# A decoder block on one core: the opening unit fed in half tiles, a fourth plain unit, the closing unit in token pieces, norms by a ones product

## The chip, the core and the metric

The kernel runs on one core of a Trainium2 chip. The metric is the device time of one execution in microseconds (us); of each kernel several executions are timed and the median is taken. One further execution is profiled, and its rows are the ones shown below.

## What is computed

One layer of a hybrid decoder block on x (2048 tokens, width 1024, float32), cut to its products and norms:

```python
u = rms_norm(h, norm1_gain)
x_lru, g_lru, q, k, v, g_ret = split(u @ w_in)            # 1024 -> 6 * 512
hl = rg_lru(causal_conv4(x_lru))                          # gates by 64x64 heads, linear scan over tokens
y_lru = rms_norm(hl * gelu(g_lru), lru_norm_gain)
y_ret = head_norm(retention(rotary(q), rotary(k), v)) * silu(g_ret)   # chunks of 128 tokens, 4 heads
h = h + concat(y_lru, y_ret) @ w_out
u = rms_norm(h, norm2_gain)
a, b = split(causal_conv3(u @ ffn_up_w))                  # 1024 -> 2 * 3072
h = h + (gelu(a) * b) @ ffn_down_w
out = rms_norm(h, final_norm_gain)                        # rms_norm: y * rsqrt(mean(y*y) + 1e-6) * gain
```

## The kernel before

Channels lie on the 128 partitions and tokens along the row. The 2048 tokens are two groups g of HT = 1024; a tile ("slot") is 128 x 1024 float32, a product tile in PSUM ("bank") 128 x 512. The work is a list of stages (`order`, line 1427): A and AS (input projection, 12 units per group), B (output projection, 4 units), U (up projection, 24 units), D (down projection, three parts of 4 units per group, the last of them D of g = 1, c = 2). A unit gives two output tiles of 128 channels by 1024 tokens.

Every float32 operand is split into two float32r parts (`split`, line 478: ScalarE casts the high part, VectorE subtracts for the low part), and each block product is three matmuls per 128 channels of contraction (wh·bh, wh·bl, wl·bh). There are two kinds of unit:

- `Unit` (line 551) does a Winograd form of Strassen: 7 products of 12 matmuls 128x512 (84 in all), with sums of weights made on VectorE and sums of data blocks read from DRAM (`Blocks`, line 365: the names 11, T1, T2, 21, T3, T4, 22).
- `PlainUnit` (line 674) does 8 products of 12 matmuls (96 in all), on blocks 11, 12, 21, 22 alone. It needs no sums. The first PLAIN = 3 units of stage A of group 0 and all of stage B are plain.

In the plain units of stage A the raw x is multiplied, with the norm's gain in the split of the block (`RawStage.bring`, line 527); the factor 1/rms of each token (`rb1`) is applied when a bank is emptied (`PlainOut.quadrant`, line 753), so no bank is emptied before `rb1` is there. Five banks (tags x, y, y, e, e) take the quadrants in turn. `norm1` (line 968) makes `rb1` from eight token-major tiles xt of x: Square with a row sum on ScalarE, a power -0.5 on GpSimd, and `spread` (line 906: a diagonal of 8 blocks on VectorE, 8 ones products on TensorE, two copies). `make_x` (line 948) then makes the normalised x and its block sums for the Winograd units.

The other norms (twice over the LRU group, twice over B's output, twice over D's) add up squares in a tile (`SumSq`, line 879) and call `rstd` (line 923): 8 products of a 128-column block with one column of ones, a VectorE step, the power on GpSimd, and `spread` again.

The order of all this is made by a planner (`Flow`, line 173). Every piece of work is a process that yields instructions with a priority, which is a due time in ticks of one product; the planner estimates when an instruction could start and fixes, for each engine, an order by readiness and priority. On the chip each engine keeps that order. SP issues all DMAs, also in that order. Slots (`SLOTS` = 50) and banks are granted by priority too; four more tiles of 128x1040 (tag "w") serve the convolutions' inputs (three or two columns of the tokens before stand ahead of them), residuals, one sum of squares, and the rotary swap. The mask and the retention states of the heads share one slot (`mst`).

At the start (`setup`, line 419) WARM = 10 products of a zero tile run on TensorE. At the end, the last unit is a Winograd unit; its two output tiles are squared, summed, and go through `rstd`, and then `normed` (line 1310) scales eight tiles of 128x1024 and sends each out.

Of the kernel before, what the change touches and what calls it, by code (L numbers as in the profile page):

```python
# [30 lines left out]
P = 128  # L31
# [9 lines left out]
W = 1040  # L41
SLOTS = 50
BANKS = {"x": 1, "y": 2, "e": 2, "sm": 3, "w": 4}
# [5 lines left out]
PLAIN = 3  # L49
SOON = 2  # L50
ISSUE = 0.45
NDUE = 0
LESS = 2
XSTEP = 5
# [3 lines left out]
LAST_PLAIN = False  # L58
WARM = 10
# [12 lines left out]
ANY_TABLE = (AF.Copy, AF.Identity, AF.Square)  # L72

# [16 lines left out]
class Engine:  # L90
# [5 lines left out]
    def __getattr__(self, op):  # L96
        fn = getattr(self.real, op)

        def describe(*args, **kw):
            aps = [x for x in list(args) + list(kw.values()) if isinstance(x, bass.AP)]  # L100
            out = kw.get("out", args[0] if args else None)
            writes = [out.tensor.name]
            if "accum_out" in kw:
                writes.append(kw["accum_out"].tensor.name)
            reads = [x.tensor.name for x in aps if x is not out]
# [67 lines left out]
class Flow:  # L173
# [27 lines left out]
    def free(self, *tiles):  # L201

        for t in tiles:
            name = t.tensor.name
            t1 = max(self.read.get(name, (0,))[0], self.wrote.get(name, (0,))[0])
            self.leaving.append((t1, self.tag.pop(name)))
# [97 lines left out]
def hymba_block_kernel(ctx: ExitStack, tc: tile.TileContext, xh, xn, win, wout, wup, down, gates, vecs,  # L304
# [7 lines left out]
    ev = ctx.enter_context(tc.tile_pool(name="ev", bufs=BANKS["w"]))  # L312
# [7 lines left out]
    def make_bank(tag, name):  # L320
        if tag == "w":
            return ev.tile([P, W], F32, tag="w", name=name)
        return ps.tile([P, Q], F32, tag=tag, name=name, bufs=BANKS[tag])

# [13 lines left out]
    def dma(dst, src):  # L338
        n = 1
        for d in dst.shape:  # L340
            n *= d
        return Op("sp", lambda: nc.sync.dma_start(dst, src), ISSUE, [dst.tensor.name], [src.tensor.name], kb=n / 256)
# [22 lines left out]
    class Blocks:  # L365
# [5 lines left out]
        def __init__(self, name):  # L371
# [35 lines left out]
    big = {}  # L407
# [20 lines left out]
    def constants():  # L428
        yield v.memset(cst, -0.5)
        mst = yield Slot("mst")  # L430
        big["msk"], big["state"] = mst[:, 0:Q], mst[:, Q:HT]
        for t in (ctail, ftail, hlast, mst[:, Q:HT]):
            yield v.memset(t, 0.0)
        for n, t, src in (("idt", idt, ident), ("sml", sml, small),
                          ("msk", mst[:, 0:Q].rearrange("p (a b) -> p a b", b=P), mask)):
            yield dma(t, src)
            have[n].on = True
        yield 0
# [28 lines left out]
    g_d = [[Blocks(f"g{g}_{c}") for c in range(3)] for g in range(NG)]  # L467
# [52 lines left out]
    class RawStage(Stage):  # L520
# [6 lines left out]
        def bring(self, name, i, need, start):  # L527
# [11 lines left out]
            else:  # L539
                hi = yield Slot("bh", F32R)  # L540
                for m in range(2):
                    yield a.activation(hi[:, half(m)], r[:, half(m)], AF.Copy, scale=col(self.gain + 4 * i + 2 * m + k))
                lo = yield Slot("bl", F32R)
                for m in range(2):
# [129 lines left out]
    class PlainUnit:  # L674
# [5 lines left out]
        count = 0  # L680

        def __init__(self, stage, wsrc, out):
            self.stage, self.wsrc, self.out = stage, wsrc, out
            self.w = {}
            self.there = [Event(), Event()]
# [8 lines left out]
        def weights(self, t0):  # L694
            self.t0 = t0

            def one(i, need):
# [6 lines left out]
                self.there[i].on = True  # L704

            fl.spawn(one(0, t0), t0 - 7)
            n1 = t0 + 2 * [m for m, n in self.quads].index(1)
            fl.spawn(one(1, n1), n1 - 7)
# [7 lines left out]
        def part(self, q, m, n, k):  # L716
# [3 lines left out]
            yield self.there[m]  # L720
            bname = f"{k + 1}{n + 1}"
            for j in range(2):
                yield self.stage.event(bname, j)
            wh, wl = self.w[m]
            op = None
            for j in range(4):
                bh, bl = self.stage.blk[bname, j // 2]
                c = half(j % 2)
                ws = slice((4 * k + j) * P, (4 * k + j + 1) * P)
                for i, (x, y) in enumerate(((wh, bh), (wh, bl), (wl, bh))):  # L730
                    mm = pe.matmul(self.ps, x[:, ws], y[:, c], start=k == 0 and j == 0 and i == 0,
                                   stop=k == 1 and j == 3 and i == 2)
                    op = op + mm if op else mm
            yield op
            self.stage.used(bname)
            if k == 1:
                if m not in [x for x, _ in self.quads[q + 1:]]:
                    free(*self.w[m])
                fl.spawn(self.out.quadrant(m, n, self.ps), self.t0 + 2 * q + 4 - SOON)


    class PlainOut:


        off = off2 = 0
        rows = ("slot", "slot")

        def tile(self, i):
            name = f"o{i}"
            t = yield (Bank("w", name) if self.rows[i] == "wide" else Slot(name))  # L750
            return t

        def quadrant(self, m, n, ps):
# [5 lines left out]
            else:  # L759
                q[m] = None  # L760
                q[m] = yield from self.tile(m)
                there.on = True
            off = (self.off, self.off2)[m] + n * Q
            if self.unit.stage.kind == "A":
                yield rb_there[self.g]
                yield v.tensor_tensor(out=q[m][:, off:off + Q], in0=ps, in1=rb1[self.g][:, half(n)], op=ALU.mult)
                rb_used(self.g)
            else:
                yield a.copy(q[m][:, off:off + Q], ps)
# [10 lines left out]
        def u2(self):  # L780
            u = self.unit
            self.t1 = yield from self.tile(0)
            yield a.copy(self.t1[:, self.off + Q:self.off + HT], u.y)
            u.done["u2"].on = True

        def c11(self):
            u = self.unit
            yield u.done["u2"]
            yield a.copy(self.t1[:, self.off:self.off + Q], u.x)
# [3 lines left out]
        def c22(self):  # L793
            u = self.unit
            self.t2 = yield from self.tile(1)
            t = self.t2[:, self.off2 + Q:self.off2 + HT]
# [6 lines left out]
        def c21(self):  # L803
            u = self.unit
            yield a.copy(self.t2[:, self.off2:self.off2 + Q], u.y)
# [4 lines left out]
        def c12(self):  # L810
            u = self.unit
            t = self.t1[:, self.off + Q:self.off + HT]
# [5 lines left out]
    class AddOut:  # L818


        def __init__(self, src, done, wide=True):
            self.src, self.done, self.wide = src, done, wide
# [3 lines left out]
        def load(self, t0):  # L826
            def fn(i):
                yield Until(t0 - 8)
                t = yield (Bank("w", "res") if self.wide else Slot("res"))
                self.t[i] = t[:, 0:HT]  # L830
# [11 lines left out]
        def quadrant(self, m, n, ps):  # L842
# [3 lines left out]
            if (m, 0) in self.quads and (m, 1) in self.quads:  # L846
                yield from self.done(m, self.t[m])

# [30 lines left out]
    class SumSq:  # L879


        def __init__(self, n, wide=False):
            self.acc, self.left, self.wide = None, n, wide

        def add(self, src):
            if self.acc is None:
                acc = yield (Bank("w", "sqacc") if self.wide else Slot("sqacc"))
                self.acc = acc[:, 0:HT]
# [657 lines left out]
```

## Time and profile before

| | us |
|---|---|
| median of 3 executions | 2239.53 (2236.61 to 2242.26) |
| the profiled execution, its time | 2237.51 |
| its span, first to last instruction | 2235.7 |
| TensorE busy in it | 2182.8 |
| VectorE busy | 1780.7 |
| ScalarE busy | 1136.8 |
| mean granted TensorE clock | 0.986 of full |

The span is measured inside the profiled execution; 1.8 us of its time lie outside the span. PE is TensorE's matmuls, PEld its weight loads, DVE VectorE, ACT ScalarE, POOL GpSimd, SPq the DMA-issuing queue of SyncE. Matmul records overlap (a 128x512 record lasts 0.39 us where the next starts 0.23 us later), so rates are read from start to start. A float32 matmul leaves two records.

### The profile page before, as it was taken

The page shows a single profiled execution, that of the slowest core. Times are in us where ns is not written, and L with a number is a line of the kernel's source. Part 1 is how long each engine was busy: PE and PEld are TensorE (multiplying, and loading weights), DVE is VectorE, ACT ScalarE, POOL GpSimd, SP SyncE. Part 2 cuts the span into 40 slices and gives each one's busy share as a digit, 9 for nine tenths or more (in the row PEclk, how much of TensorE's full clock was granted, in tenths as well). Part 3 has the DMA queues.
Part 4 walks back from the last instruction along what each step waited for, and adds up shares of the span by engine and source line. Part 5 has one row for each costly group of instructions (what it writes and reads, how often), then busy time and mean ns, then how long its engine had stood idle before and what let it go on. Part 6 is the DMA issues. An engine that isn't in the chain of part 4 may idle for free.

```text
span 2235.7 us, 26267 instructions
## 1 busy us (share of the span) xinstructions
PE 2182.8 (98%) x9880; PEld 1796.9 (80%) x9880; DVE 1780.7 (80%) x2266; ACT 1136.8 (51%) x1578; POOL 39.7 (2%) x28
## 2 busy tenths in 40 slices
PE   8998999999999999999999999999999999999996
PEld 6877778888788888888888878888888788887884
DVE  7988779777675688899878897878788887788775
ACT  5674666565633155555555755555556444434431
POOL 0000000000000000000000000000000000000000
PEclk9999999999999999999999999999999999999998
DMA  9955263322646872445323532323226677679641
GB/s 356 340 187 196 94 228 135 97 97 94 193 176 238 302 270 95 156 159 179 113 94 137 207 114 99 112 100 102 99 100 224 216 268 285 242 288 370 242 181 75
DMA packets 136063, 405.90 MB, mean 182 GB/s; under 512 B 15232, under 2 KB 16512, under 8 KB 135936
## 3 DMA queue, kind: packets, MB, share of 16 engines
q1 hardware_dynamic: 135936, 404.23, 51.3%
q8 instruction: 77, 1.26, 0.2%
q14 instruction: 50, 0.41, 0.1%
HBM read 272.04 MB, written 123.73 MB: 177 GB/s over the span
## 4 chain that ended last, share of the span: by engine, by line
PE 91%; DVE 4%; DMA 2%; ACT 2%; issue 0%; SPq 0%; POOLq 0%; DVEq 0%; ACTq 0%
PE py L111 33%; PE px L111 22%; PE pe L111 21%; PE pq L111 10%; PE po L111 1%; PE sc L111 1%; DVE res L111 1%; PE pt L111 1%; DVE wl L111 1%; DMA w<-in_dram 1%; PE pk L111 1%; PE pb L111 1%; PE mst L111 0%; PE pa L111 0%; PE pg L111 0%; DVE o L111 0%
## 5 line engine op out<-in xcount | busy, mean ns | idle before, releaser
L111 PE MATMUL py<-bh,wh 128*128 128x512 f32 x744 | 292.8, 394 | 8.4 <-ACT wh L111 6.8
L111 PE MATMUL pe<-bh,wh 128*128 128x512 f32 x744 | 296.6, 399 | 1.0 <-DVE o L111 1.0
L111 PE MATMUL py<-bh,wl 128*128 128x512 f32 x744 | 292.1, 393 | 3.6 <-DVE wl L111 3.6
L111 PE MATMUL px<-bh,wl 128*128 128x512 f32 x744 | 290.6, 391 | 2.3 <-DVE wl L111 2.3
L111 PE MATMUL px<-bh,wh 128*128 128x512 f32 x744 | 291.9, 392 | 0.5 <-DVE res L111 0.5
L111 PE MATMUL pe<-bl,wh 128*128 128x512 f32 x744 | 291.6, 392 | 0.7 <-DVE bl L111 0.7
L111 PE MATMUL pe<-bh,wl 128*128 128x512 f32 x744 | 291.6, 392 | 0.0
L111 PE MATMUL py<-bl,wh 128*128 128x512 f32 x744 | 291.4, 392 | 0.0
L111 PE MATMUL px<-bl,wh 128*128 128x512 f32 x744 | 289.9, 390 | 0.0
L111 ACT CAST wh<-s 128x1024 fp32r<-128x1024 f32 x186 | 195.5, 1051 | 151.2 <-DVE s L111 130.6
L111 DVE SCALAR_TENSOR_TENSOR c<-o,vec,c 128x1024 f32<-128x1024 f32 x192 | 245.9, 1282 | 15.7 <-ACT c L111 12.8
L111 PE MATMUL py<-bh,wv 128*128 128x512 f32 x744 | 248.8, 395 | 3.4 <-ACT bh L111 1.9
L111 DVE TENSOR_TENSOR wl<-s,wh 128x1024 fp32r<-128x1024 f32 x186 | 227.0, 1220 | 29.1 <-ACT wh L111 15.2
L111 ACT COPY o<-py 128x512 f32<-128x512 f32 x207 | 121.5, 587 | 194.2 <-PE py L111 184.9
L111 DVE TENSOR_TENSOR bl<-raw,bh 128x1024 fp32r<-128x1024 f32 x156 | 186.6, 1219 | 2.8 <-ACT bh L111 2.8
L111 ACT ACTIVATE c<-o,vec 128x1024 f32<-128x1024 f32 x96 | 119.7, 1247 | 130.7 <-DVE o L111 130.7
L111 ACT CAST bh<-raw 128x1024 fp32r<-128x1024 f32 x156 | 159.9, 1049 | 40.8 <-DMA raw<-g_T 10.1
L111 PEld LDWEIGHTS py<-bh,wh 128*128 128x128 f32 x744 | 140.7, 189 | 39.5 <-ACT wh L111 8.1
L111 PEld LDWEIGHTS py<-bh,wl 128*128 128x128 f32 x744 | 140.7, 189 | 35.2 <-DVE wl L111 5.8
L111 PEld LDWEIGHTS py<-bh,wv 128*128 128x128 f32 x744 | 140.7, 189 | 34.8 <-ACT bh L111 2.3
L111 PEld LDWEIGHTS pe<-bh,wh 128*128 128x128 f32 x744 | 141.0, 190 | 31.4 <-issue 1.7
L111 PEld LDWEIGHTS pe<-bl,wh 128*128 128x128 f32 x744 | 141.0, 189 | 31.4 <-issue 1.7
(135 smaller groups left out, 3744.2 us busy)
## 6 DMA issues: line engine op xcount, KB each, us to landing
wa<-in_dram SPq DMA_DIRECT2D x93, 512.0 KB, 4.3
wb<-in_dram SPq DMA_DIRECT2D x93, 512.0 KB, 4.3
h<-res SPq DMA_DIRECT2D x56, 512.0 KB, 3.9
g_T<-t SPq DMA_DIRECT2D x96, 256.0 KB, 2.5
raw<-g_T SPq DMA_DIRECT2D x48, 512.0 KB, 6.6
res<-h SPq DMA_DIRECT2D x48, 512.0 KB, 4.6
g<-c SPq DMA_DIRECT2D x72, 256.0 KB, 3.5
raw<-g SPq DMA_DIRECT2D x36, 512.0 KB, 6.8
```

What stands on the lines that cost most here:

```text
L111: return Op(self.name, lambda: fn(*args, **kw), us, writes, reads, func=func)
```

## The change

- Opening: of the first unit, the first weight tile is loaded and split in halves, the wait for blocks stands ahead of each half block, and instructions go out per half block. The second block tile is asked for before the split. The xt loads are due three ticks later (NDUE 0 to 3), constants at tick 3 instead of -5, softplus at 6 instead of 0; warm-up products fall from 10 to 3. The loads of `make_x` no longer wait for `rb1`.
- PLAIN 3 to 4: the fourth unit of stage A of group 0 (its second LRU unit) is plain.
- Closing: the last unit is a `LastUnit`: a plain unit in token ranges 0-512, 512-768, 768-1024. Each range is added, squared, summed, normalised and sent out on its own.
- `rstd`: two float32 products of a 128x128 ones tile with the sum of squares (128x512 each), a ScalarE Sqrt, a VectorE reciprocal.
- All tiles are slots: SLOTS 50 to 54, the four wide tiles go. The convolutions work on 1024 columns and correct the first two or three columns separately (UpOut: three ACT instructions on one column instead of one copy; LruOut: three more small VectorE instructions, one copy less). The mask is one 128x128 tile, the states pass from group 0 to group 1 through DRAM, the gate weights lie in the slot of `ea`.
- The planner knows halves of tiles (`parts`); SOON 2 to 1.5, XSTEP 5 to 6.

```diff
-SLOTS = 50
-BANKS = {"x": 1, "y": 2, "e": 2, "sm": 3, "w": 4}
+SLOTS = 54
+BANKS = {"x": 1, "y": 2, "e": 2, "sm": 3}
-PLAIN = 3
-SOON = 2
+PLAIN = 4
+SOON = 1.5
-NDUE = 0
+NDUE = 3
-XSTEP = 5
+XSTEP = 6
+XD0 = 6
-WARM = 10
+WARM = 3
...
             def part(i, need, k, r, hi, lo):
+                yield dma(r[:, half(k)], self.wsrc[i][:, half(k)])
+                yield need - 2
+                yield a.copy(hi[:, half(k)], r[:, half(k)])
+                yield low(lo[:, half(k)], r[:, half(k)], hi[:, half(k)])
+                self.there[i][k].on = True
...
+            if self.halves:
+                fl.spawn(first(0, t0), t0 - 9)
...
+    class LastUnit(PlainUnit):
+        ranges = ((0, 512), (512, 768), (768, 1024))
+        quads = tuple((m, r) for r in ranges for m in range(2))
...
     def rstd(ss, n, out):
-        rt = sp.tile([P, NCH], F32, tag="ms", name="ms")
-        pm = yield Bank("sm", "mst")
...
-        yield p.tensor_tensor(out=rt, in0=rt, in1=cst.to_broadcast([P, NCH]), op=ALU.pow)
-        yield from spread(rt, out)
+        r = yield Slot("rb")
+        for i in range(2):
+            pm = yield Bank("sm", "mst")
+            yield pe.matmul(pm, ones, ss.acc[:, half(i)], start=True, stop=True)
+            yield a.activation(r[:, half(i)], pm, AF.Sqrt, scale=1.0 / n, bias=eps)
+            free(pm)
+            yield v.reciprocal(r[:, half(i)], r[:, half(i)])
         free(ss.acc)
+        out.append(r)
...
         def one(q):
-            yield rb_there[g]
             yield Until(start + XSTEP * q)
...
+            yield rb_there[g]
             for j in range(2):
                 yield v.scalar_tensor_tensor(out=t[j], in0=t[j], scalar=col(V_N1 + 2 * q + j), in1=rb1[g], ...)
...
+    class FinalGroup(NormGroup):
+        def piece(self, m, t, c0, c1):
+            self.t[m] = t
+            q = yield Slot("sqt")
+            yield a.activation(q[:, 0:c1 - c0], t[:, c0:c1], AF.Square)
+            acc = self.ss.acc[:, c0:c1]
+            yield v.tensor_tensor(out=acc, in0=acc, in1=q[:, 0:c1 - c0], op=ALU.add)
+            free(q)
+            self.count = getattr(self, "count", 0) + 1
+            if self.count % 2 == 0:
+                pm = yield Bank("sm", "mst")
+                yield pe.matmul(pm[:, 0:c1 - c0], ones, acc, start=True, stop=True)
+                r = yield Slot("rb")
+                r = r[:, 0:c1 - c0]
+                yield a.activation(r, pm[:, 0:c1 - c0], AF.Sqrt, scale=1.0 / D, bias=eps)
+                yield v.reciprocal(r, r)
+                for k in range(KT):
+                    y = self.t[k][:, c0:c1]
+                    yield v.scalar_tensor_tensor(out=y, in0=y, scalar=col(V_NF + k), in1=r, op0=ALU.mult, op1=ALU.mult)
+                    fl.spawn(self.out(k, y, c0, c1), 10 ** 6)
...
         def conv(self, e, f):
-            yield a.copy(e[:, 0:2], ftail[:, f])
...
+            for i, k, w in ((0, 0, w0), (0, 1, w1), (1, 1, w0)):
+                yield a.activation(c[:, i:i + 1], ftail[:, f, k:k + 1], AF.Identity, bias=c[:, i:i + 1], scale=w)
+            yield a.copy(ftail[:, f], e[:, HT - 2:HT])
...
-        fl.spawn(constants(), -5)
+        fl.spawn(constants(), 3)
```

## Rows read from the trace of the kernel before

**Rows 1.** The page: busy time and share of the span of each engine.

```profile
PE 2182.8 (98%) x9880; PEld 1796.9 (80%) x9880; DVE 1780.7 (80%) x2266; ACT 1136.8 (51%) x1578; POOL 39.7 (2%) x28
```

**Rows 2.** Waits of PE: who waited for whom, us in total, times, longest.

```profile
PE mst L111 <- DVE sqacc L111: 7.0, 3, 3.4
...
PE pq L111 <- ACT bh L111: 4.7, 1, 4.7
```

**Rows 3.** Timeline, PE in the opening: start, us, what, idle before it.

```profile
1.59 11.26 PE L111 MATMUL y<-z,ones 128*128 128x512 f32 x20 [1.59 <-DVE z L111]
...
17.56 0.79 PE L111 MATMUL pq<-bh,wh 128*128 128x512 f32 x1 [4.71 <-ACT bh L111]
...
18.94 0.63 PE L111 MATMUL pq<-bh,wl 128*128 128x512 f32 x1
...
19.36 0.63 PE L111 MATMUL pq<-bh,wh 128*128 128x512 f32 x1
...
23.60 0.40 PE L111 MATMUL pq<-bl,wh 128*128 128x512 f32 x1
```

**Rows 4.** Timeline, ACT in the opening.

```profile
13.77 1.06 ACT L111 ACTIVATE xt<-xt 128x1024 f32<-128x1024 f32 x1 [6.06 <-DMA xt<-in_dram]
...
28.74 1.05 ACT L111 ACTIVATE xt<-xt 128x1024 f32<-128x1024 f32 x1
...
36.27 0.59 ACT L111 COPY rb<-pb 128x512 f32<-128x512 f32 x1 [0.25 <-PE pb L111]
```

**Rows 5.** DMA of the first 40 us: GB/s in forty slices of 1 us.

```profile
GB/s 0 46 208 336 414 291 356 361 340 332 344 283 342 412 402 404 344 393 385 412 422 414 397 404 412 422 395 391 406 389 395 406 399 434 385 397 434 393 393 410
```

**Rows 6.** Timeline, DVE: the first two banks emptied.

```profile
38.76 1.29 DVE L111 TENSOR_TENSOR o<-pq,rb 128x512 f32<-128x512 f32 x2
```

**Rows 7.** The chain that ended last, in order of time: start, us, what.

```profile
64.22 0.86 PE pa L111 x2
...
89.52 0.44 PE pt L111 x4
...
2200.35 2.73 PE py L111 x12
```

**Rows 8.** Timeline, PE around the norm's column sums at 728 us.

```profile
728.16 1.84 PE L111 MATMUL mst<-ones,sqacc 128*128 128x1 f32 x16
729.86 0.49 PE L111 MATMUL pq<-bh,wh 128*128 128x512 f32 x1
```

**Rows 9.** Timeline of the end.

```profile
2209.28 0.39 PE L111 MATMUL pe<-bh,wl 128*128 128x512 f32 x1
...
2213.11 1.92 PE L111 MATMUL mst<-ones,sqacc 128*128 128x1 f32 x16 [3.45 <-DVE sqacc L111]
...
2221.89 9.66 DVE L111 SCALAR_TENSOR_TENSOR res<-res,vec,rb 128x1024 f32<-128x1024 f32 x8 [3.19 <-ACT rb L111]
```

**Rows 10.** DVE and ACT groups by shape: count, busy us, mean ns, idle before.

```profile
L111 DVE TENSOR_TENSOR res<-res,pe 128x512 f32<-128x512 f32 x48 | 32.9, 686 | 15.3 <-PE pe L111 14.4
...
L111 DVE SCALAR_TENSOR_TENSOR st<-st,pk 128x128 f32<-128x128 f32 x56 | 16.0, 287 | 6.8 <-PE pk L111 5.3
...
L111 DVE TENSOR_TENSOR spl<-spl 128x4 f32<-128x4 f32 x10 | 1.6, 161 | 0.3
...
L111 DVE RECIPROCAL spl<-spl 128x4 f32<-128x4 f32 x1 | 0.2, 178 | 0.0
...
L111 ACT COPY o<-py 128x512 f32<-128x512 f32 x207 | 121.5, 587 | 194.2 <-PE py L111 184.9 <-DVE xc L111 6.2 <-DMA gat<-in_dram 2.1
...
L111 ACT COPY o<-ftail 128x2 f32<-128x2 f32 x96 | 18.2, 190 | 0.0
```

**Rows 11.** Windows: us, busy by engine (PE, PEld, DVE, ACT, POOL), PEclk, DMA, GB/s.

```profile
160.00:180.00 20.00, 13.66 (x53) 10.55 (x51) 19.06 (x21) 5.72 (x7) 0.00 (x0) 0.91 0.59 213
180.00:200.00 20.00, 18.42 (x89) 15.14 (x90) 16.89 (x22) 7.09 (x12) 0.00 (x0) 0.83 0.67 228
```

**Rows 12.** Timeline, ACT before that stall.

```profile
151.52 1.28 ACT L111 ACT_TABLE_LOAD   x1 [3.67 <-DMA x<-x]
```

More of the change, by code (lines that the diff above doesn't have):

```diff
@@ L72, with parts @@
 ANY_TABLE = (AF.Copy, AF.Identity, AF.Square)
+def parts(ap):
+    name = ap.tensor.name
+    if ap.ap[0][0] != HT:
+        return [name]
+    lo = ap.offset % HT
+    hi = lo + sum((n - 1) * step for step, n in ap.ap[1:])
+    return [f"{name}.{i}" for i in range(lo // Q, hi // Q + 1)]
 class Op:
@@ L684, in __init__ @@
             self.w = {}
-            self.there = [Event(), Event()]
+            self.there = [[Event(), Event()] for m in range(2)]
             self.placed = [Event(), Event()]
@@ L719, in part @@
                 self.ps = yield Bank(self.tags[PlainUnit.count % 5], "pq")
-            yield self.there[m]
+            yield self.there[m][k]
             bname = f"{k + 1}{n + 1}"
-            for j in range(2):
-                yield self.stage.event(bname, j)
             wh, wl = self.w[m]
@@ L742, in hymba_block_kernel, with leave, products, __getattr__ @@
-    class PlainOut:
[L745 to L751, printed above, removed]
+                fl.spawn(self.leave(m, n, c0, c1), self.t0 + 2 * q + 4 - SOON)
+        def leave(self, m, n, c0, c1):
+            return self.out.quadrant(m, n, self.ps)
+    class LastUnit(PlainUnit):
+        ranges = ((0, 512), (512, 768), (768, 1024))
+        quads = tuple((m, r) for r in ranges for m in range(2))
+        @property
+        def products(self):
+            res, dt = [], 0
+            for q, (m, (c0, c1)) in enumerate(self.quads):
+                for k in range(2):
+                    res.append((dt, f"q{2 * q + k}", f"{k + 1}{c0 // Q + 1}"))
+                    dt += (c1 - c0) / Q
+            return res
+        def __getattr__(self, name):
+            if name[0] != "q" or not name[1:].isdigit():
+                raise AttributeError(name)
+            q, k = divmod(int(name[1:]), 2)
+            m, (c0, c1) = self.quads[q]
+            return lambda: self.part(q, m, c0 // Q, k, c0, c1)
+        def leave(self, m, n, c0, c1):
+            return self.out.piece(m, c0, c1, self.ps)
@@ L781, in u2 @@
             u = self.unit
-            self.t1 = yield from self.tile(0)
-            yield a.copy(self.t1[:, self.off + Q:self.off + HT], u.y)
+            self.t1 = yield Slot("o0")
+            yield a.copy(self.t1[:, half(1)], u.y)
             u.done["u2"].on = True
@@ L794, in c22 @@
             u = self.unit
[L795 to L796 removed]
+            self.t2 = yield Slot("o1")
+            t = self.t2[:, half(1)]
             yield a.copy(t, u.y)
@@ L847, in quadrant, with piece @@
                 yield from self.done(m, self.t[m])
+        def piece(self, m, c0, c1, ps):
+            yield self.there[m]
+            t = self.t[m][:, c0:c1]
+            yield v.tensor_tensor(out=t, in0=t, in1=ps[:, 0:c1 - c0], op=ALU.add)
+            free(ps)
+            yield from self.pieces(m, self.t[m], c0, c1)
         def u2(self):
```

198 lines of the change are left out of this document (107 added, 91 removed).

## Prediction

> **What bounds the kernel now.** I read the page first. PE is busy 98% of the span, DVE 80%, ACT 51% [rows 1]: the matmuls are the bound, and the other engines matter where PE waits for them. PE's waits come next. All of them together are 53 us of 2235.7, and the reader is to see that they are few and local: 7.0 us in three places for sums of squares, 4.7 us once for the first block [rows 2]. So there are four ways to gain: begin earlier, end sooner after the last matmul, give PE less to do, stall less between.
>
> In the opening PE does warm-up products from 1.59 to 12.85, idles 4.71 us, begins real work at 17.56, and then matmuls follow each other at 0.42 us (18.94 to 19.36), which is 512 columns at 1.2 GHz [rows 3]. In the steady state twelve take 2.73 us, 0.2275 each, the 2.4 GHz level [rows 7]. The slow records (0.63 us long, against 0.40) end at 23.60 [rows 3]: thirteen matmuls take 6.0 us where 3.0 would do, some 2.8 of it the clock's, the rest a wait for the first low part. ACT shows why PE began late: its queue held the first xt square, ready at 13.77, ahead of the first block [rows 4]. Banks are emptied from 38.76 on [rows 6], after the rb copy at 36.27 [rows 4].
>
> **Opening.** I add up the bytes against the delivered rate [rows 5]: 1.0 MB have come by 5 us, 5.2 by 17, 10.1 by 29. The first weight half and first half block are 0.92 MB with the vectors: in by 4.8 us, then a cast and a subtraction. A float32 product is two records of 0.43 us at 2.4 GHz (the pa pair [rows 7]) and so 0.86 each at 1.2; three warm-up products keep PE to about 6.7 us if they all run cold, and the first real matmul follows there instead of at 17.56. The constants' three loads and softplus's two dozen small DVE instructions (0.16 us each [rows 10]), moved behind, cost nothing; the LRU gates that need them come later. The second weight is in with 3.28 MB at 12 us and split by 14.2, so PE waits 2 us there at most; blocks 12 and 22 (5.4 MB, 17.5 us) are in before they are used. Two of the unit's eight products are done by then; six of 2.73 us follow from 14.5, so the unit ends at about 31 and the fifth quadrant, of the next unit, at 36.4. There the five banks are full.
>
> Moved behind the blocks are eight xt loads and eight squares. They are in with 10.2 MB, at 29.4 us; the last square ends at 30.7 instead of 29.7 [rows 4], and the chain from there to rb took 7.2 us, so rb stands at about 38 and the first bank is free at 39.4. PE idles 3 us and I charge the slow spell of 2.8 again. The sixth quadrant starts in effect at 42.2; before, it was 17.56 + 120 x 0.2275 + 2.8 + 0.45 = 48.1. **Gain 6**, with ends 12 (rb in time) and 2 (rb four us later still). The x loads of `make_x`, no longer behind rb, are eight DMAs due after xt, so they take no bandwidth from it; they only hold eight slots earlier.
>
> **Fourth plain unit.** 96 matmuls in place of 84: 12 x 0.2275 = **2.7 lost** [rows 7]. DVE sheds its four weight sums and one split there, some 3 us, and the transformed blocks are due one unit later.
>
> **Norms.** Before, each `rstd` takes PE 1.70 us for the column sums (728.16 to 729.86) [rows 8] and 16 records of 128 columns in `spread`, at 0.11 each (four in 0.44 [rows 7]) 1.75 us. After, two float32 products of 512 columns, 0.86 us each (the pa pair [rows 7] is two records of one product), 1.72 us. That saves 1.73 us in each of five norms inside the PE-bound stretch: **8.7 gained**. Where PE sits waiting for the sum anyway this is smaller (3 of them: no less than 4). On DVE two reciprocals replace eight diagonal steps. DVE keeps its order, so a reciprocal that waits for the root (0.86 + 0.6 us) holds the weight splits behind it; DVE waited for the power before, so I charge nothing.
>
> The trace has no reciprocal of this size. By shape the nearest row is an add of 128x512, 0.69 us; by operation it is the 128x4 reciprocal, 178 ns against 161 for a product of that size, 17 ns over four columns, which carried to 512 columns is 0.69 + 2.2 = 2.9 us [rows 10]. I take 2.9, the same operation, and keep 0.69 as the other end; as the excess is near what two equal records differ by, twice the excess (5.1) is the far end. The Trainium skill, page "VectorE: DVE Perf Modes", section "First, the fixed hardware budget", says that the reciprocal runs as an iterative divide with a repeat count of 8; if every column takes eight steps at the add's slope, an estimate by that page is 4.4 us, and the sum would come out about 3 us higher at the end of the kernel. No run here shows it yet.
>
> **Closing unit.** Before, the last matmul starts at 2209.28 and the span ends at 2235.7: 26.2 us after it, made of the last squares to 2213.11, column sums, power and spread to 2221.89, and eight steps of 1.2 us with the last transfer behind [rows 9]. After, PE does 48 matmuls of 512 columns (10.9 us) and 96 of 256. The 256-column float32r matmul is not in the trace: the bounds are 0.106 (the column sums, where only weight loads limit: 1.70/16 [rows 8]) and 0.2275. I take 0.12, near the low end, because columns halve and weight loads do not bind above 0.106. That is 22.4 us against 84 x 0.2275 = 19.1: 3.3 lost, and 10.3 more at the upper bound. Two of the three ones products (0.86 + 0.43) fall before the last matmul: 1.3 lost.
>
> The tail by parts, 256 columns wide (DVE slope 1.04 ns from 287 ns at 128 and 686 at 512 columns, so 0.42; ACT 0.4 from 587 at 512 [rows 10]): add, square, add, product 0.43, root, reciprocal 1.5, eight steps at about 0.34, a 128 KB store of some 2.5 (the 512 KB one took 4.1, from the last step's end at 2231.6), joints of 0.7: 10 us. DVE is behind, though: range 0 gets its reciprocal (2.9) and eight steps of 0.6 from 16 us into the unit, ends at 23.7, range 1 at 29.5, range 2 at 33.7, store to 36.5; PE ends at 23.7. So the tail is 12.8 instead of 26.2: **13.4 gained**, less 4.6: 8.8 net. Ends 12 and 0.
>
> **Tiles.** Four wide tiles become four slots; the memory is the same and one slot (mask and states) comes free. UpOut has two more small ACT instructions in each of 96 convolutions, 192 x 0.19 = 36 us [rows 10]; ACT is idle half the span [rows 1], so they cost nothing, and 36 at most if that cover were gone. LruOut: 2.6 us of DVE in all. States through DRAM: eight 64 KB transfers with four units' lead.
>
> **Stalls between.** Another plan moves every stall. The largest, in group 1's LRU units, is two windows in which PE is busy 13.66 and 18.42 of 20 us at clocks 0.91 and 0.83 [rows 11]: 7.9 idle and (0.09 + 0.17) x 20 = 5.2 of clock, 13 us. It begins when ACT waits 3.67 us for a store of x to release a tile [rows 12]; the LRU chain runs late and DVE's weight splits behind it. With slots no longer reserved for one use I take back **4** of the 13; the bounds are 25 either way, which is what PE idles in all between the opening and the tail (53 less 6 and some 20).
>
> **Sum.** -6 + 2.7 - 8.7 - 8.8 - 4 = -24.8 against the profiled execution's 2237.5: 2212.7. The median of the runs shown is 2.0 above that execution, so I predict 2215.
>
> **Rivals.**
> 1. *The wait for rb takes the place of the wait for the block.* PE fills five banks and stands longer; the opening gains 2 or nothing, giving 2219 to 2221. For it: the xt bytes move back by 1.3 MB. Against: 9 us of slack were there before (five quadrants from 17.56 end near 48, the first bank was emptied at 38.76). Chance 0.17.
> 2. *The reciprocal holds DVE.* At 5.1 us per half, DVE gives 4.4 us more to each norm, PE stands at three of them with the clock falling in turn (3 x 4), and the tail grows by 4: 2215 + 16 = 2231. For it the 17 ns; against it that three splits of slack lie ahead of most stages. Chance 0.12. By itself, the Trainium skill's page "VectorE: DVE Perf Modes" (section "First, the fixed hardware budget") stands on this rival's side, at the lower price given above.
> 3. *Slots run short in stage A* (the slower side). The eight early x tiles, the LRU inputs and residuals now compete with weights. Each wait like that of [rows 12] becomes a stall of 13 us. It decides from two new ones on (25/13); with three, 2215 + 39 = 2254. For it: the one now; against: one slot more in all and less DVE work at the plain unit. Chance 0.1.
> 4. *The stalls mostly go*, those of group 1 and the two at norms: 20 less, 2195. Chance 0.13.
>
> That the half-tile steps do nothing because an instruction waits for whole tiles is excluded by the opening: PE started at 17.56, when only the first half cast from 16.8 had ended.
>
> **How the numbers follow.** The forecast case has 0.48. The range 2195 to 2236 holds it, rivals 1, 2 and 4, and the 256-column bound; it leaves out rival 3 and half of what lies below rival 4. A measurement here tells 0.3% (6.7 us) from no change, that is 2232.8 and 2246.2. Faster: 0.46 + 0.15 + 0.07 + 0.13 = 0.81; same 0.1; slower 0.09.
>
> **What would show it.** First pq matmul near 7 us; a wait of pq for o near 36 to 39 us; no mst and pb groups except norm1's; ones products of 0.86 a pair; 256-column matmuls 0.12 apart; the reciprocal's own record; the last matmul 13 us before the end; the stretch from the sixth quadrant to the last unit some 14 us shorter plus the fourth unit's 2.7. The forecast is wrong if rb comes after 42 us, if 256-column matmuls stand 0.2 apart, or if PE's waits between 60 and 2180 us exceed the present ones by over 15 us.

## The result and the profile after

The kernel after takes 2223.2 us (median of four runs, 2222.4 to 2223.4), the one before, run beside it, 2238.4 (2236.6 to 2242.3). The ratio is 0.9929, with an interval of 0.9912 to 0.9946: 15 us faster, where 2215 (24 faster than its median) was predicted. The profiled execution has a span of 2221.6 us, 14.1 less than before. First the engines and the waits of PE (who waited for whom, us in total, times, longest), which answer to [rows 1, 2].

```profile
PE 2165.6 (97%) x9772; PEld 1776.6 (80%) x9772; DVE 1805.9 (81%) x2250; ACT 1237.3 (56%) x1773; POOL 25.9 (1%) x22
```

```profile
PE py L122 <- DVE wl L122: 9.0, 6, 4.1
PE py L122 <- ACT wh L122: 8.8, 5, 3.7
PE pt L122 <- DVE o L122: 6.7, 2, 5.1
...
PE mst L122 <- DVE sqacc L122: 3.5, 3, 2.2
```

PE has shed 17.2 us and DVE gained 25.2. ACT gained 100; 83 of it come from the convolutions, where 288 instructions on one column stand in place of 96 small copies [rows 10] (groups of ACT: count, busy us, mean ns):

```profile
L122 ACT ACTIVATE c<-ftail,c,vec 128x1 f32<-128x1 f32 x288 | 101.2, 382 | 4.2
```

They stand between 824 and 1736 us, where PE is busy 545.25 of the 546 us from 740 to 1286 and 440.00 of the 440 from 1300 to 1740; its longer waits between are 1.76 us for a cast of ACT at 1288.97 and 1.13 behind it. So ACT's new work cost little. The wait for the first block has gone from the top of the list, that for the sums of squares has halved, and a new one stands there: 5.1 us in one place for a transposed tile (pt) that DVE had not finished.

**Opening.** The timeline of PE, beside [rows 3]:

```profile
1.59 5.49 PE L122 MATMUL y<-z,ones 128*128 128x512 f32 x6 [1.59 <-DVE z L122]
7.73 0.51 PE L122 MATMUL pq<-bh,wh 128*128 128x512 f32 x1 [0.65 <-ACT bh L122]
...
9.10 0.40 PE L122 MATMUL pq<-bh,wh 128*128 128x512 f32 x1
9.33 0.39 PE L122 MATMUL pq<-bl,wh 128*128 128x512 f32 x1
...
36.84 1.95 PE L122 MATMUL pb<-dg,ones 128*128 128x128 f32 x16
39.30 0.50 PE L122 MATMUL pq<-bh,wh 128*128 128x512 f32 x1 [0.51 <-DVE o L122]
```

Real work begins at 7.73 instead of 17.56, and matmuls stand 0.23 apart from about 9 on: the stretch at the lower clock is gone. The fifth quadrant ends at 36.84. There PE does the products of `spread` for the first norm, then waits 0.51 us for a bank, and the sixth quadrant (the 121st matmul of the plain units) starts at 39.30. In the kernel before it starts 11.1 us later (timeline of PE):

```profile
50.45 0.39 PE L111 MATMUL pq<-bh,wh 128*128 128x512 f32 x1
```

**Between.** A norm's ones product in the dense stretch costs what was reckoned: it starts at 722.72, the second matmul behind it at 723.81, and a quadrant's matmuls stand 0.23 apart, which leaves 0.86 (timeline of PE, beside [rows 8]).

```profile
722.72 1.02 PE L122 MATMUL mst<-sqacc,ones 128*128 128x512 f32 x2
...
723.81 0.40 PE L122 MATMUL pq<-bl,wh 128*128 128x512 f32 x1
```

Its reciprocal is the surprise. By shape, the groups of DVE (count, busy us, mean ns):

```profile
L122 DVE RECIPROCAL rb<-rb 128x512 f32<-128x512 f32 x11 | 36.7, 3342 | 0.3 <-ACT rb L122 0.3
L122 DVE RECIPROCAL rb<-rb 128x256 f32<-128x256 f32 x2 | 3.5, 1748 | 0.0
```

(3342 - 1748)/256 is 6.2 ns a column, six times an add's slope of 1.04 [rows 10]. At the norm near 316 us it meets the tile for which PE waits. DVE's timeline, then PE's:

```profile
316.40 3.35 DVE L122 RECIPROCAL rb<-rb 128x512 f32<-128x512 f32 x1
319.66 1.16 DVE L122 TENSOR_TENSOR o<-o,rope 128x1024 f32<-128x1024 f32 x1
...
321.99 1.23 DVE L122 TENSOR_TENSOR o<-o,sw 128x1024 f32<-128x1024 f32 x1
323.13 3.35 DVE L122 RECIPROCAL rb<-rb 128x512 f32<-128x512 f32 x1
```

```profile
323.27 1.97 PE L122 MATMUL pt<-idt,o 128*128 128x128 f32 x8 [5.12 <-DVE o L122]
```

DVE has no gap here. The first reciprocal stands ahead of the three rope steps, and PE waits for the last of them; how much of the 5.12 us is the reciprocal's is measured in experiment 1. Where PE stalls in this way the granted clock is lower too. The windows (PE, PEld, DVE, ACT, POOL busy, PEclk, DMA share, GB/s), beside [rows 11]:

```profile
160.00:180.00 20.00, 19.06 (x90) 15.56 (x89) 18.06 (x22) 8.78 (x13) 0.00 (x0) 1.00 0.74 249
320.00:340.00 20.00, 16.73 (x80) 14.53 (x81) 19.96 (x21) 11.26 (x15) 0.00 (x0) 0.83 0.35 126
380.00:400.00 20.00, 17.30 (x69) 14.18 (x70) 18.36 (x19) 8.27 (x12) 0.00 (x0) 0.91 0.53 161
1980.00:2000.00 20.00, 15.06 (x53) 11.10 (x53) 18.42 (x18) 1.74 (x3) 0.00 (x0) 0.83 0.64 216
```

The stall at 160 that was 13 us before has nearly gone; PE stops 5.12, 4.08 and 3.67 us elsewhere (323, 383 and 1991 us).

**Closing.** The timeline of DVE from the first reciprocal of the last unit on; the last matmul starts at 2203.98, beside [rows 9].

```profile
2196.40 3.35 DVE L122 RECIPROCAL rb<-rb 128x512 f32<-128x512 f32 x1 [0.26 <-ACT rb L122]
2199.79 5.39 DVE L122 SCALAR_TENSOR_TENSOR res<-res,vec,rb 128x512 f32<-128x512 f32 x8
...
2207.98 1.75 DVE L122 RECIPROCAL rb<-rb 128x256 f32<-128x256 f32 x1
2209.77 3.25 DVE L122 SCALAR_TENSOR_TENSOR res<-res,vec,rb 128x256 f32<-128x256 f32 x8
2212.95 1.74 DVE L122 RECIPROCAL rb<-rb 128x256 f32<-128x256 f32 x1
2214.72 3.26 DVE L122 SCALAR_TENSOR_TENSOR res<-res,vec,rb 128x256 f32<-128x256 f32 x8
```

```profile
2203.86 0.28 PE L122 MATMUL pq<-bl,wh 128*128 128x256 f32 x1
2203.98 0.28 PE L122 MATMUL pq<-bh,wl 128*128 128x256 f32 x1
```

The tail is 17.6 us instead of 26.4 (from the start of the last matmul), with DVE at work almost without a gap up to 2217.98 and the last stores behind it; matmuls of 256 columns stand 0.12 apart.

### The profile page after: what moved, and what is told of

Its sections match the earlier page's. It is cut to its first block, busy times and chain, and to the rows that moved or that the text cites. A ratio compares the mean times of both kernels' runs of the same rounds, so it can differ in the third digit from the quotient of the medians.

```text
span 2221.6 us, 26370 instructions
## 1 busy us (share of the span) xinstructions
PE 2165.6 (97%) x9772; PEld 1776.6 (80%) x9772; DVE 1805.9 (81%) x2250; ACT 1237.3 (56%) x1773; POOL 25.9 (1%) x22
## 4 chain that ended last, share of the span: by engine, by line
PE 89%; DVE 6%; ACT 2%; DMA 1%; issue 1%; SPq 0%; DVEq 0%; ACTq 0%
PE py L122 32%; PE px L122 21%; PE pe L122 20%; PE pq L122 12%; PE po L122 1%; DVE rb L122 1%; DVE res L122 1%; DVE o L122 1%; PE pk L122 1%; PE sc L122 1%; DVE bl L122 1%; PE pt L122 1%; DVE wl L122 1%; PE pa L122 1%; PE pg L122 0%
## 5 line engine op out<-in xcount | busy, mean ns | idle before, releaser
L122 PE MATMUL py<-bh,wh 128*128 128x512 f32 x728 | 289.9, 398 | 12.8 <-ACT wh L122 8.8
L122 PE MATMUL pe<-bh,wh 128*128 128x512 f32 x728 | 287.4, 395 | 1.6 <-DVE o L122 1.6
L122 PE MATMUL pe<-bl,wh 128*128 128x512 f32 x728 | 283.7, 390 | 2.2 <-DVE bl L122 2.1
L122 PE MATMUL px<-bh,wh 128*128 128x512 f32 x728 | 285.3, 392 | 0.0
L122 PE MATMUL pe<-bh,wl 128*128 128x512 f32 x728 | 283.6, 390 | 0.1
L122 PE MATMUL px<-bh,wl 128*128 128x512 f32 x728 | 283.5, 389 | 0.0
L122 PE MATMUL px<-bl,wh 128*128 128x512 f32 x728 | 283.3, 389 | 0.0
L122 DVE SCALAR_TENSOR_TENSOR c<-o,vec,c 128x1022 f32<-128x1022 f32 x192 | 245.3, 1279 | 13.8 <-ACT c L122 8.3
L122 PEld LDWEIGHTS py<-bh,wh 128*128 128x128 f32 x728 | 139.3, 191 | 44.9 <-ACT wh L122 10.9
L122 PE MATMUL pq<-bh,wh 128*128 128x512 f32 (+1 forms) x432 | 168.5, 390 | 1.2 <-ACT bh L122 0.7
L122 PE MATMUL pq<-bl,wh 128*128 128x512 f32 (+1 forms) x432 | 165.2, 382 | 0.7 <-DVE bl L122 0.7
L122 PE MATMUL pq<-bh,wl 128*128 128x512 f32 (+1 forms) x432 | 165.0, 382 | 0.5 <-DVE wl L122 0.5
```

What stands on the lines that cost most here:

```text
L122: return Op(self.name, lambda: fn(*args, **kw), us, writes, reads, func=func)
```

## The experiments

Each kernel is the kernel after with one edit, or one group of edits, timed in five rounds against the kernel before. The runs were made in three sessions beside that of the kernel after, in which the median of the kernel before lay between 2237.0 and 2238.9; the ratios allow for that, the differences of medians named below do not (by the ratios 7 is 11 us slower than after and 12 is 31). The intervals of 2, 4 and 8 overlap with that of after, but every run of these three is slower than every run of after. The table gives the median, the ratio to before with its interval, the start of the last matmul and the tail from there to the span's end in the profiled execution.

| kernel | us | ratio | last matmul | tail |
|---|---|---|---|---|
| after | 2223.2 | 0.9929 (0.9912 to 0.9946) | 2204.0 | 17.6 |
| 1 reciprocal as a product | 2204.7 | 0.9847 (0.9830 to 0.9864) | 2191.0 | 12.9 |
| 2 closing unit undone | 2229.2 | 0.9956 (0.9940 to 0.9972) | 2201.0 | 26.8 |
| 3 three plain units | 2235.5 | 0.9981 (0.9972 to 0.9990) | 2216.6 | 17.6 |
| 4 opening undone | 2228.8 | 0.9956 (0.9941 to 0.9971) | 2209.3 | 17.6 |
| 5 small reciprocal at the end | 2222.4 | 0.9926 (0.9914 to 0.9939) | 2205.6 | 14.7 |
| 6 small reciprocals everywhere | 2215.5 | 0.9894 (0.9880 to 0.9907) | 2194.9 | 14.7 |
| 7 SOON 2 | 2232.4 | 0.9979 (0.9969 to 0.9990) | 2215.0 | 17.6 |
| 8 planner told the price | 2226.5 | 0.9944 (0.9930 to 0.9957) | 2207.4 | 17.6 |
| 9 logarithm and exponential | 2208.4 | 0.9865 (0.9852 to 0.9879) | 2190.4 | 17.8 |
| 10 the same, small end | 2207.3 | 0.9868 (0.9855 to 0.9881) | 2188.0 | 16.3 |
| 12 fifty slots | 2250.4 | 1.0066 (1.0052 to 1.0079) | 2230.1 | 17.6 |

**1. What the reciprocal's length costs.** The order of all instructions stays; each reciprocal behind the first norm becomes a product.

```diff
-            yield v.reciprocal(r[:, half(i)], r[:, half(i)])
+            yield v.tensor_tensor(out=r[:, half(i)], in0=r[:, half(i)], in1=r[:, half(i)], op=ALU.mult)
...
-                yield v.reciprocal(r, r)
+                yield v.tensor_tensor(out=r, in0=r, in1=r, op=ALU.mult)
```

> The changed kernel with each reciprocal replaced by a product of the same tile with itself: the reciprocals are left out, so the norms come out wrong in value; the planner gives both the same price (0.69 us at 512 columns), so the order of all instructions stays the same and only DVE's time for these 13 instructions falls, from 3.34 and 1.75 us to about 0.69 and 0.42. Theory A (the reciprocal's price holds DVE, at the end and at the norms between): 5.3 us less at the end (2.65 + 1.33 + 1.33), and the PE waits of 5.1 us at 323 and 4.8 us at 1991 with their slow spells of 3.4 each go, so 15 to 22 us less than the changed kernel's 2223: 2201 to 2208, ratio to before 0.984 to 0.987. Rival B (the waits between come from the order, not from the price): only the end gains, 2218, ratio 0.991.

18.5 us faster than after. The steps of 512 columns take 685 ns (groups of DVE), those of 256 421 ns, the transposes' wait shrinks from 5.12 to 2.50, and the 3.67 at 1990.86 is gone (timeline of PE):

```profile
L122 DVE TENSOR_TENSOR rb<-rb 128x512 f32<-128x512 f32 x11 | 7.5, 685 | 2.7 <-ACT rb L122 2.7
```

```profile
320.77 1.09 PE L122 MATMUL pt<-idt,o 128*128 128x128 f32 x8 [2.50 <-DVE o L122]
379.48 0.80 PE L122 MATMUL py<-bh,wl 128*128 128x512 f32 x1 [4.08 <-DVE wl L122]
```

DVE has 31.9 us less to do (11 x 2.66 + 2 x 1.33). The last matmul starts 13.0 us earlier and the tail is 4.7 shorter. From the sixth quadrant to the last matmul PE idles 27.2 us instead of 36.4 and is busy 4.0 less with the same matmuls, which is the clock's part. So the reciprocal's length delays the matmuls by 13.0, by way of stalls and the clock behind them, and lengthens the end by 4.7. Set matmul against matmul (tile px), the lead arises at four of the five norms: 3.4 us at the one of 316 us, 2.5 at that of 611, 1.4 at that of 842 and 6.5 at that of 1974. At the one of 721 it is nothing, though two reciprocals stand back to back there: DVE had been busy 6.42 of the 20 us before, and PE is busy without a break from 720 to 740. The 4.08 us stall for wl stays and is not the reciprocal's.

**2. The closing unit by itself.**

```diff
-            kind = LastUnit if final and m == KT // 2 - 1 else Unit
+            kind = Unit
...
-        ng = FinalGroup(V_NF, None) if final else NormGroup(V_NF, store, h_d[g][3])
+        ng = NormGroup(V_NF, store, None if final else h_d[g][3])
```

> The changed kernel with the last unit as before (a Winograd unit, eight tiles of 1024 columns normalised behind it), the new norm kept. Theory A (the traces: tail 26.2 us before, 17.6 after, 4.6 us more work for PE, so the closing unit is worth 4): 2227, ratio 0.995, with the end some 26 us after the last matmul. Rival B (it is worth the 8.8 that were forecast): 2232, ratio 0.997.

6.0 us slower than after, between the two. The tail is 9.2 longer; the last matmul comes 2.9 earlier. DVE's timeline of the end:

```profile
2207.68 6.57 DVE L122 RECIPROCAL rb<-rb 128x512 f32<-128x512 f32 x2 [2.94 <-ACT rb L122]
2214.28 9.66 DVE L122 SCALAR_TENSOR_TENSOR res<-res,vec,rb 128x1024 f32<-128x1024 f32 x8
```

**3. The fourth plain unit by itself.**

```diff
-PLAIN = 4
+PLAIN = 3
```

> The changed kernel with PLAIN = 3. Theory A (the fourth plain unit buys DVE time: PE begins 9 us earlier while the normalised blocks come no earlier, so with three plain units the first Winograd unit waits for blocks): 2226 to 2232, PE waiting 5 us or more for bl or wl between 85 and 180 us. Rival B (it only adds 12 matmuls): 2.7 us less, 2220.5.

12.3 us slower, more than was expected: the unit that costs PE twelve more matmuls is a gain. PE waits not for a block but for the first state of a head (8.72 us, and 1.12 for the next), and at 243.43 for a weight (wv, 4.83 us). The timelines of PE and DVE show the first:

```profile
95.85 0.77 PE L122 MATMUL po<-st,o 128*128 128x128 f32 x2 [8.72 <-DVE st L122]
```

```profile
91.28 1.22 DVE L122 TENSOR_TENSOR wl<-s,wh 128x1024 fp32r<-128x1024 f32 x1
...
94.15 0.68 DVE L122 TENSOR_TENSOR s<-s,wa 128x512 f32<-128x512 f32 x1
...
95.54 0.17 DVE L122 MEMSET st<- 128x128 f32 x1
```

DVE works here without a gap, and the weight sums and splits of a transformed fourth unit (s, wl, bl) stand ahead of the first state, which PE needs. The state's MEMSET uses none of their results; it is late because DVE keeps the planned order. PE is busy 9.83 of the 20 us from 80 on at a clock of 0.72; in the kernel after it is 20.00 at 1.00.

**4. The opening undone**, with warm-up, loads and constants as before. What stays is the planner's knowledge of halves, the wait for blocks ahead of each half block, the order in which a block's two tiles are asked for, and the due times of `make_x` (XD0, XSTEP).

```diff
-        us[0].halves = True
-NDUE = 3
+NDUE = 0
-WARM = 3
+WARM = 10
...
-        fl.spawn(constants(), 3)
+        fl.spawn(constants(), -5)
```

> The changed kernel with the opening as before: whole weight tiles, no half steps, xt loads due at once, constants early, ten warm-up products, x loads behind rb; four plain units kept. Theory A (the sixth quadrant began at 39.3 instead of 48.1 and that lead is kept to the end): 9 us more, 2232, ratio 0.997. Rival B (the lead is lost again to DVE before 200 us): within 3 us of the changed kernel, 2223 to 2226.

5.6 us slower than after, between the two. Its first real matmul starts at 11.95, PE waits 3.34 us for the first norm's diagonal at 29.46, and the sixth quadrant starts at 46.71, 7.4 us behind after. The px matmuls that after has at 175.62 and 303.84 come 8.0 to 8.1 us later here, the one at 330.18 and all behind it 5.6 to 5.3 (timeline of PE):

```profile
311.88 0.39 PE L122 MATMUL px<-bh,wh 128*128 128x512 f32 x1
...
329.17 1.12 PE L122 MATMUL pt<-idt,o 128*128 128x128 f32 x4 [4.50 <-DVE o L122]
...
335.79 0.39 PE L122 MATMUL px<-bh,wh 128*128 128x512 f32 x1
```

So 2.4 of the 8.0 us that the opening has won by then are given back at the norm near 316, where PE waits for DVE in both kernels, longer in the one that comes earlier (5.12 us against 4.50).

**5 and 6. A reciprocal of a few columns**, with the column sums, diagonal and ones products of before: in the closing unit alone, where the scaling reads the result from PSUM (5), and in the five norms between as well (6).

```diff
-                yield pe.matmul(pm[:, 0:c1 - c0], ones, acc, start=True, stop=True)
+                for t in range(nt):
+                    o = pe.matmul(pm[:, t:t + 1], blk(acc, t), ones[:, 0:1], start=True, stop=True)
...
+                yield a.activation(rt[:, 0:nt], pm[:, 0:nt], AF.Sqrt, scale=1.0 / D, bias=eps)
+                yield v.reciprocal(rt[:, 0:nt], rt[:, 0:nt])
+                dg = yield from diagonal(rt, nt)
```

> The changed kernel, but the three ranges of the closing unit take root and reciprocal on one column per 128 tokens (column sums, 128x4 or 128x2), and spread the result with a diagonal and ones products that the scaling reads from PSUM; the norms between stay. Theory A (DVE is the bound of the closing stretch, so its time counts in full): reciprocals fall from 6.8 us to 0.5, eight diagonal steps of 0.2 come in, 4.6 us off DVE, one more hop of about 1 us at the very end: 3 to 4.5 less, 2219 to 2220, ratio 0.9915. Rival B (the longer chain of hops or the SP queue's stores take its place): no gain, 2222 to 2224.

> As the run before it, and the five norms between take root and reciprocal on 128x8 too (column sums, diagonal, spread as in the kernel before, but with root and reciprocal for the power). DVE is rid of 26 us more, PE does 1.75 us more in each of five norms. Theory A (the waits near the norms come from DVE's 3.3 us blocks): 13 us of waits go as in the run with products, 8.7 come back as PE work, and the end gains 3 to 4.5: 2214 to 2217. Rival B (a new order brings its own waits): 2219 or more.

At the end alone it brings nothing that can be told from after (2222.4, intervals overlap): the tail is 2.9 shorter, but the last matmul is 1.6 later. The joints take the reciprocal's place, as DVE's timeline of 5 shows: 0.16 and 0.48 us of work, then a wait for PE.

```profile
2211.59 0.16 DVE L122 RECIPROCAL ms<-ms 128x2 f32<-128x2 f32 x1
2211.78 0.48 DVE L122 TENSOR_SCALAR dg<-idt,ms 128x128 f32<-128x128 f32 x2
2213.45 3.22 DVE L122 SCALAR_TENSOR_TENSOR res<-res,vec,pb 128x256 f32<-128x256 f32 x8 [1.18 <-PE pb L122]
```

In all norms it brings 7.7 (runs from 2211 to 2218; the profiled one is the fastest), of which the five norms between make 7.0, as 5 has the same end. PE has its 128-column records back in them, so there DVE's time is dearer than PE's.

**8. Was it the order alone?** The planner reckons a reciprocal at 0.69 us; here it is told the measured length.

```diff
+        if op == "reciprocal":
+            return 0.14 + 6.25e-3 * n
```

> The changed kernel with one line more in the planner's price list: the reciprocal costs 0.14 us and 6.25 ns a column (3.34 at 512), where it was reckoned at 0.69. The instructions are the same, only the order may change. Theory A (the waits come because the order was made for a reciprocal five times cheaper): half or more of the 13 us of waits go, 2213 to 2218. Rival B (DVE lacks the time, whatever the order): 2221 to 2225.

3.3 us slower than after, outside both. The wait has moved and grown (timeline of PE):

```profile
325.83 1.97 PE L122 MATMUL pt<-idt,o 128*128 128x128 f32 x8 [8.88 <-DVE o L122]
```

So in this planner a better estimate did not help; what helped was to take the work off DVE (1, 6, 9 and 10).

**9 and 10. Off DVE.** exp(-0.5 ln(mean + eps)) on ACT in place of root and reciprocal, in every norm behind the first (9); in 10 the two halves' logarithms come first and one exponential of 1024 columns follows, with the end of experiment 5.

```diff
-            yield a.activation(r[:, half(i)], pm, AF.Sqrt, scale=1.0 / n, bias=eps)
-            yield v.reciprocal(r[:, half(i)], r[:, half(i)])
+            yield a.activation(r[:, half(i)], pm, AF.Ln, scale=1.0 / n, bias=eps)
+            yield a.activation(r[:, half(i)], r[:, half(i)], AF.Exp, scale=-0.5)
```

> The changed kernel with the reciprocal square root made on ACT alone, as exp(-0.5 ln(mean + eps)), in all norms behind the first; DVE has no part in it, the ones products stay. Theory A (DVE's reciprocals are worth what the run with products showed, 18.5 us): ACT gets 0.7 us a half and a few table loads of 1.28, DVE gives 1.4 us a norm less than in that run: 2202 to 2207, ratio 0.983 to 0.986. Rival B (table loads on ACT delay the weight casts behind them): 2210 or more, with PE waiting for ACT wh near 320, 610 and 1990.

> The log and exp form for the five norms between, with both halves' logs ahead of one exp of 1024 columns, so that each norm needs two table loads instead of four, and the small root and reciprocal in the closing unit. Theory A (table loads and the end each cost the run before a few us): 2 to 5 less than its 2208, so 2203 to 2207, ratio 0.985. Rival B (rb comes later because the exp waits for both halves, and PE waits for it): 2208 to 2213.

2208.4 and 2207.3, the same within their intervals, some 15 below after and 30 below before: the best versions here that keep the reciprocal root. 9 falls just outside the 2202 to 2207 expected of it, and 10 between its two theories. The wait at 323 is down to 1.92. What stands between 9 and experiment 1 (2204.7) is on ACT, whose timeline of 9 shows a table load ahead of each function:

```profile
314.93 1.28 ACT L122 ACT_TABLE_LOAD   x1
316.23 0.69 ACT L122 ACTIVATE rb<-mst,eps 128x512 f32<-128x512 f32 x1
316.94 1.28 ACT L122 ACT_TABLE_LOAD   x1
318.23 0.63 ACT L122 ACTIVATE rb<-rb 128x512 f32<-128x512 f32 x1
```

In the stages the loads do no harm: the last matmul of 9 starts 0.7 us earlier than that of 1. In the tail they stand in the chain: DVE waits 3.52 and 3.09 us for rb, and the tail is 17.8 us long, 5.0 longer than that of 1. The Trainium skill, page "ScalarE: Activation LUTs", section "Table sets: the hidden batching unit", has logarithm and exponential in one table set, one load for both. By that the second load of each pair would not be there; the program of 9 does not bear it out, with 70 loads against 47 in the kernel after.

**7. The order's constant by itself.** SOON sets by how many ticks the steps behind a unit's matmuls fall due earlier.

```diff
-SOON = 1.5
+SOON = 2
```

> The changed kernel with SOON = 2 as before, everything else as changed: banks are emptied half a tick more eagerly. It measures how far a change of order alone moves the time. Theory A (the order moves single waits by a few us, with no trend): within 5 us of 2223 on either side. Rival B (the constant itself is worth more than that): outside 2218 to 2228.

9.2 us slower, outside what was expected. Set against the kernel after, PE's waits come later and later up to 627 us and by an even amount from there on (timeline of PE; after has these three at 323.27, 615.83 and 1749.83):

```profile
328.69 1.73 PE L122 MATMUL pt<-idt,o 128*128 128x128 f32 x8 [2.21 <-DVE o L122]
...
626.67 0.66 PE L122 MATMUL pt<-idt,o 128*128 128x128 f32 x4 [2.56 <-DVE o L122]
...
1760.69 0.50 PE L122 MATMUL pe<-bl,wh 128*128 128x512 f32 x1 [1.80 <-DVE bl L122]
```

The lags are 5.4, 10.8 and 10.9. In the window from 380 to 400 us PE is busy 12.25 us at a clock of 0.74, against 17.30 at 0.91 in the kernel after. Which instruction's place in the order decides it the runs do not show.

**12. The four slots by themselves.**

```diff
-SLOTS = 54
+SLOTS = 50
```

> The changed kernel with SLOTS = 50 instead of 54, that is four equal buffers fewer and 2 MB of SBUF unused. Theory A (buffers limit stage A, where the early x tiles, LRU inputs and weights compete): 2230 or more, with longer PE waits between 85 and 400 us. Rival B (54 is more than is needed at the places where PE waits): within 3 us of 2223.

27.2 us slower than after, and slower than before. The kernel before had four wide tiles beside its 50 slots, so this kernel has four tiles fewer than either. PE's longer waits begin at 175 us (4.30 there, 3.18 at 236.51, 4.97 at 321.73). Near 630 us PE now waits for a sum of squares that DVE made late, and DVE and ACT had waited for loads (timelines of PE, DVE and ACT):

```profile
635.04 2.08 PE L122 MATMUL mst<-sqacc,ones 128*128 128x512 f32 x2 [6.27 <-DVE sqacc L122]
```

```profile
629.56 1.23 DVE L122 TENSOR_TENSOR o<-o,rope 128x1024 f32<-128x1024 f32 x1 [2.91 <-DMA sw<-o]
```

```profile
631.73 1.04 ACT L122 CAST bh<-raw 128x1024 fp32r<-128x1024 f32 x1 [5.08 <-DMA raw<-m]
```

The lag to after is 18.4 us at the transposes of 323, some 12 between 390 and 460, and 27.8 at those of 616; all of it arises up to there. That these loads were issued late for want of a slot fits the edit, but no row names the slot.

## Why the prediction was right, and where it was off

Faster was right, and the time lies inside the range, 8 us above the forecast. That it lies so near is in part luck. By the profiled executions 14.1 us were gained where 24.8 were forecast: the lead at the sixth quadrant is 5.2 larger than forecast, the stretch from there to the last matmul 11.3 worse, the tail 4.6 worse.

- **Opening: right in mechanism, too small in size.** The first real matmul was put at 6.7 and came at 7.73. The fifth quadrant was to end at 36.4 and the first bank to be free at 39.4; PE got there at 36.84 and went on at 39.30. Two terms failed. The slow spell of 2.8 at the full banks did not come: PE did 1.95 us of `spread` products there, idled 0.51, and the granted clock is 1.00 from 38 to 44 us. And the 48.1 for the kernel before was reckoned without the same products and not read: the trace has 50.45. So the lead there is 11.1 us, not 6. The clock of the first matmuls did not decide it: in the execution of experiment 1 PE paused 1.98 us behind the warm-up, the granted clock was 0.51 from 8 to 10 us, and the sixth quadrant still began at 39.52. Rival 1 is out. But a lead at 40 us is not a gain at the end: undoing the opening cost 7.4 us there and 5.6 at the end.
- **Fourth plain unit: the sign was wrong.** It was charged with 2.7 lost, and the 3 us that DVE sheds were counted as nothing. Those DVE steps stand ahead of the first state, and without the fourth plain unit PE waits 8.72 us for it: the unit is worth 12 in this kernel.
- **Norms: PE's share right, DVE's wrong.** 0.86 us a product, as reckoned. "I charge nothing" for DVE is the step that failed: experiment 1 shows 13.0 us of delay up to the last matmul, more than the 8.7 that the term promised, and with the old form in these five norms (6 against 5) the kernel is 7.0 us faster. The price was taken as 2.9 us and measured 3.34; the clue of the 128x4 row pointed the right way. The Trainium skill's page "VectorE: DVE Perf Modes" (section "First, the fixed hardware budget") gives the repeat count of 8 from which 4.4 was estimated. The trace does not bear that estimate out: a column costs six times an add's, not eight. Rival 2 named this mechanism and then asked 5.1 us of it before it counted; it counted at 3.34, at four of the five norms.
- **Closing: right in kind, 3 us too much.** Net 8.8 was forecast, 6.0 measured by experiment 2. On PE it costs 2.9 (4.6 forecast; 0.12 us for 256 columns was exact; one ones product falls before the last matmul, not two). The tail was to be 12.8 and is 17.6. DVE is the bound there, as said, and the term that was short is its work: three reciprocals (6.8 us instead of 5.9) and eight and sixteen steps of 0.67 and 0.41 instead of 0.6 and 0.34, 2.6 us together; then 1.2 more in the additions between the first two ranges and 0.8 at the last store. With the reciprocals as products the tail is 12.9.
- **Tiles: the price was wrong, the cover right.** ACT was charged with 36 us more for the convolutions and has 83: a one-column instruction with two column operands takes 382 ns, not the 190 of a small copy. ACT had the room for it, as said: PE's waits near 1289 (2.9 us) are the only long ones in that stretch.
- **Stalls between: the sign was wrong.** The stall at 160 us has nearly gone, as hoped. In its place are those at 134, 323, 383 and 1991. From the sixth quadrant (11.1 ahead) to the last matmul (5.3 ahead) 5.8 us of the lead is lost, where by the forecast 2.7 and 4.6 of PE's work are added and 8.7 taken away: 1.4 of gain on paper, so 7.2 of stalls came where 4 were to go. PE idles 36.4 us in this stretch, 25.8 in the kernel before.
- **What had no term.** SOON is worth 9 us and four slots 27 in this kernel; the prediction gave slots a part of the 4 and SOON nothing. Rival 3 (slots run short) did not come true, and experiment 12 shows how near it lay.

The parts do not add up: undone one at a time, the opening, the fourth unit, the closing unit, SOON and the slots cost 5.6, 12.3, 6.0, 9.2 and 27.2, some 60 together, and the change as a whole is worth 15. Each was undone with the rest in place, where a late DVE or a missing buffer may cost more than it did in the kernel before. Which of them would help the kernel before by itself was not tried; nor were the due times of `make_x` and the new form of the convolutions undone by themselves.

## What to carry to other kernels

Before work goes from a busy engine to a less busy one, look for its gaps in the stage in question. DVE was at 80% in the whole. Where it had a gap (721 us) two long reciprocals cost nothing; where it had none (1974 us) they cost 6.5 us on PE, with the clock's loss in it. A long instruction is priced by its own kind and its columns: a reciprocal belongs on few columns, or on an idle engine in another form. A constant of the plan or a few buffers can outweigh the change that came with them, so try these alone first. And a time of the kernel before is read from its trace, not reckoned.

## What was not expected of the hardware

- A float32 reciprocal costs 3.34 us at 128x512, 1.75 at 128x256 and 0.18 at 128x4.
- Right behind 5.49 us of warm-up products and a pause of 0.65 us the clock was at its upper level: the granted clock is 1.00 from 8 to 10 us, and matmuls of 512 columns stood 0.23 apart from about 9 us on. In the kernel before, behind 11.26 us of them and a pause of 4.71, it is 0.53 from 17 to 24 us.
- An ACT instruction on one column took 382 ns where scale, bias and source are columns, and a copy of two columns 190.
- In the program of 9 logarithm and exponential each brought their own table load of 1.28 us, even back to back.
